# attn x v: v loaded in rows of 32 KiB, sixteen heads at a time, and spread in front of the transposes

## The chip, the core and the metric

One core of a Trainium2 chip runs the whole program. The metric is the time of one execution in microseconds (us) on the device. The kernel before took 1050.37 us, the median of three runs (1050.12 to 1050.52).

Names used below: TensorE (PE) multiplies matrices and transposes them by a matmul against an identity; its weight loads are PEld. VectorE (DVE) and ScalarE (ACT) copy results out of PSUM. GpSimd (POOL) issues most transfers here, and SyncE (SP) the others. [...]

## The reference

```python
# attn_weights: (8, 12, 1024, 1024) float32, v: (8, 12, 1024, 64) float32
np.einsum('bhqs,bhsd->bhqd', attn_weights, v).astype(np.float32)
```

For each of 96 heads a 1024 x 1024 matrix is multiplied with a 1024 x 64 one. `attn` is 403 MB, v and the output 25 MB each.

## The kernel before

**Tiling.** Four heads make one step of the loop, 24 steps in all (`NV`). In a tile of 128 partitions each of the four heads has 32 partitions, and a partition holds 32 consecutive query rows of its head. A step is two *units* of 16 of these rows each (`G` = 16, `NU` = 48 units): the even one (`i == 0`) and the odd one. A unit's part of `attn` is 8 MB in float32, loaded by one transfer on POOL that casts it to bfloat16 on the way (`load_attn`, L344), 64 KiB to a partition, into one of two buffers `abf`.

**A unit on TensorE** (`pe_unit`). It waits for its load and transposes the 16 groups by 64 matmuls (`transpose_g`, L144), two bfloat16 taken as one float32, into four PSUM banks in turn. Copies on DVE (ten groups) and ACT (six) bring them to `at` (L277); a group waits for the copy of the group four before it. Then `transpose_back` (L174) transposes the output `ot` of the unit before by eight matmuls into the banks `px`, from where ACT copies it to `osb` (L258). Then 64 matmuls (L189) form the products of `at` with v (`vbf`) in the banks `po`, and DVE and ACT copy them to `ot` (L289).

**v and its spreading.** The products need v with the sequence on the partitions in an interleaved order. v comes in long rows: with `V8` = 8 heads on 128 partitions, a partition holds 64 consecutive rows of one head, 16 KiB in float32. `spread_v` brings them into place by matmuls against a band matrix `spread`: step b of `VB` = 8 takes the row block b of all 16 partitions of a head and puts it on every eighth partition. It accumulates the steps of a head in one PSUM bank (`po` and `px`, one bank a head); the contraction runs over 32 partitions (`VR`), in which two heads lie, and the other head's weights are zero. The four heads of a step lie on two sets of 32 partitions. The steps are written in pairs of heads, (0, 2) and then (1, 3), so that each matmul is followed by one on the other set. Each head has its own band in `spread`. DVE and ACT cast the four results to `vbf` (L250).

**The order.** All of it is written by hand, engine by engine, with semaphores. In an even unit TensorE transposes `attn` first, then waits for the copies of the products of the unit before (`s_ot`) and for v (`s_vr`), spreads, waits for the four casts (`s_vbf`), transposes back and multiplies. A branch on the loop's counter picks the spread for the step's place in the buffer `vr`.

**Transfers.** POOL issues in program order. Before the loop: the first unit of `attn`, a part of the first v, the second unit. In the loop: in the even unit, where a load of v is due (`V_LOADS`: eight heads for step 2, then sixteen heads for steps 4, 8, ..., 20), it waits for the spread that read the old v last (`s_sp`) and issues that load (L350). Then in each unit it waits until the unit's transposes are done (`s_t`) and issues the `attn` load after next into the buffer that these freed. The first v comes in two halves, one by SP through `osb` with a cast on DVE (L332), one by POOL. Stores of `osb` come in two bursts, after steps 8 and 16, and at the end; TensorE halts half-way through unit 18 and unit 34 until a burst has landed (`s_half`).

## Time and profile before

| | |
|---|---|
| time, median of three runs | 1050.37 us |
| span of the profiled execution | 1048.8 us |
| PE busy | 792.7 us, 76% of the span |
| PEld, DVE, ACT busy | 706.1, 389.3, 469.5 us |
| mean granted TensorE clock | 0.879 |
| HBM read, written | 427.82 MB, 25.17 MB |
| loads of `attn`, 4096 KB landed each | 46, median 29.2 us from issue to landing |
| loads of v, 2048 KB landed each | 5, median 15.8 us |
| spreading (L161), matmuls | 768, TensorE busy 87.0 us |

The profiled execution is read by its span, from its first instruction to its last; what the runs' times have beyond it (1.6 us at the median) lies around that. In a group of the profile stand the line, engine and operation, the shapes, the count, the busy time, the mean length of one instruction in ns, and the idle time just before the group with what ended it. Matmuls overlap in the pipeline, so their mean length times their count is more than their busy time. In the timeline and the chain of waits a row begins with start and length in us.

### The profile page before, as it was taken

Reading aid. Unit: us, or ns where it says so; the run is one execution under the profiler, and the core shown is the slowest. Engines: PE = TensorE matmul, PEld = TensorE weight load, DVE = VectorE, ACT = ScalarE, POOL = GpSimd, SP = SyncE. Lnnn points to the kernel's source line nnn. Section 1 sums busy time; section 2 is a strip of 40 time slices with the busy share of each in tenths; the row PEclk is TensorE's granted clock in tenths of the full one; section 3 lists DMA queues with packets and bytes.
Section 4 is the critical chain, followed back from the end, with each engine's and each line's share of the span. In section 5 each row is a group of like instructions: output and inputs, shape, how many; then the busy total and the mean of one; then the engine's idle time right before and its main releaser. Section 6 shows DMA issues by size and latency. Waiting matters only on the chain.

```text
span 1048.8 us, 17363 instructions
## 1 busy us (share of the span) xinstructions
PE 792.7 (76%) x7304; PEld 706.1 (67%) x7304; DVE 389.3 (37%) x584; ACT 469.5 (45%) x590; POOL 36.9 (4%) x68
## 2 busy tenths in 40 slices
PE   0978788479889393888949789748578884987994
PEld 0777687368778383777838588647567774867884
DVE  1443344234435151343515344324324332533542
ACT  0445355244545251354526355434335443544553
POOL 1000000000000000000000000000000000000000
PEclk9989799798999697889979899988778987998998
DMA  9999999999999999999999999999999999999999
GB/s 216 226 220 217 217 209 217 220 220 216 220 215 207 221 220 379 217 219 210 212 223 220 216 220 217 206 221 220 319 237 219 214 209 223 220 217 219 210 214 400
DMA packets 10662, 239.68 MB, mean 229 GB/s; under 512 B 1056, under 2 KB 1056, under 8 KB 1184
## 3 DMA queue, kind: packets, MB, share of 16 engines
q0 software_dynamic: 10080, 232.26, 98.9%
q1 hardware_dynamic: 576, 7.34, 1.7%
q8 instruction: 3, 0.05, 0.0%
q14 instruction: 3, 0.02, 0.0%
HBM read 427.82 MB, written 25.17 MB: 432 GB/s over the span
## 4 chain that ended last, share of the span: by engine, by line
DMA 71%; PE 26%; issue 1%; POOL 1%; ACT 0%; DVE 0%; SPq 0%; ACTq 0%; POOLq 0%
DMA abf<-in_attn_weights_dram 63%; PE bank L144 22%; DMA out_dram<-osb 8%; PE bank L161 3%; PE bank L189 1%; PE bank L174 0%; POOL vr L350 0%; DVE osb L258 0%; ACT vbf L250 0%; ACT osb L258 0%; POOL abf L344 0%; ACT ot L289 0%; POOL out_dram L358 0%; ACTq L258 0%; SPq L420 0%
## 5 line engine op out<-in xcount | busy, mean ns | idle before, releaser
L144 PE MATMUL bank<-ident,abf 128*128 128x128 f32 x3072 | 428.8, 307 | 213.0 <-DMA abf<-in_attn_weights_dram 189.5
L144 PEld LDWEIGHTS bank<-ident,abf 128*128 128x128 f32 x3072 | 419.1, 212 | 224.7 <-DMA abf<-in_attn_weights_dram 197.7
L277 DVE COPY at<-bank 128x1024 bf16<-128x1024 bf16 x480 | 319.6, 689 | 401.8 <-PE bank L144 395.2
L277 ACT COPY at<-bank 128x1024 bf16<-128x1024 bf16 x288 | 287.9, 1012 | 328.6 <-PE bank L144 328.6
L189 PE MATMUL bank<-at,vbf 128*64 128x256 bf16 x3072 | 225.5, 285 | 0.0
L189 PEld LDWEIGHTS bank<-at,vbf 128*64 128x64 bf16 x3072 | 203.6, 111 | 19.1 <-issue 6.1
L258 ACT COPY osb<-bank 64x512 f32 (+1 forms) x194 | 112.4, 580 | 28.1 <-PE bank L174 25.5
L289 DVE COPY ot<-bank 128x512 f32<-128x512 f32 x48 | 33.2, 692 | 207.1 <-PE bank L189 207.1
L161 PE MATMUL bank<-vr,spread 32*128 32x512 bf16 x768 | 87.0, 375 | 0.5 <-issue 0.2
L289 ACT COPY ot<-bank 128x512 f32<-128x512 f32 x48 | 28.1, 585 | 129.2 <-PE bank L189 129.2
L174 PE MATMUL bank<-ident,ot 128*128 128x128 f32 x392 | 61.3, 307 | 29.3 <-ACT vbf L250 28.7
L174 PEld LDWEIGHTS bank<-ident,ot 128*128 128x128 f32 x392 | 50.3, 157 | 41.4 <-ACT vbf L250 40.5
L161 PEld LDWEIGHTS bank<-vr,spread 32*128 32x128 bf16 x768 | 35.2, 93 | 43.9 <-issue 1.6
L250 ACT CAST vbf<-bank 128x512 bf16<-128x512 f32 x48 | 25.8, 588 | 74.3 <-PE bank L161 74.3
L344 POOL DMA_DIRECT2D abf<-in_attn_weights_dram x50 | 26.9, 537 | 816.1 <-PE bank L144 815.3
L250 DVE CAST vbf<-bank 128x512 bf16<-128x512 f32 x48 | 30.9, 686 | 29.1 <-PE bank L161 29.1
L277 ACT ACT_TABLE_LOAD x12 | 15.4, 1283 | 6.4 <-DMA osb<-in_v_dram 6.3
L350 POOL DMA_DIRECT2D vr<-in_v_dram x6 | 4.0, 675 | 132.9 <-PE bank L161 132.9
L358 POOL DMA_DIRECT2D out_dram<-osb x5 | 3.1, 620 | 7.5 <-ACT osb L258 7.5
L258 DVE COPY osb<-bank 64x512 f32<-64x512 f32 x2 | 1.4, 688 | 3.0 <-PE bank L174 3.0
L325 DVE MEMSET ident<- 128x128 f32 x1 | 0.2, 165 | 6.2 <-DMA osb<-in_v_dram 6.2
L332 DVE CAST vr<-osb 128x1024 bf16<-128x1024 f32 x2 | 2.2, 1138 | 0.0
(9 smaller groups left out, 5.1 us busy)
## 6 DMA issues: line engine op xcount, KB each, us to landing
abf<-in_attn_weights_dram POOLq DMA_DIRECT2D x46, 4096.0 KB, 29.2
vr<-in_v_dram POOLq DMA_DIRECT2D x5, 2048.0 KB, 15.8
out_dram<-osb POOLq DMA_DIRECT2D x1, 8192.0 KB, 39.5
abf<-in_attn_weights_dram POOLq DMA_DIRECT2D x4, 2048.0 KB, 22.8
out_dram<-osb POOLq DMA_DIRECT2D x3, 2048.0 KB, 32.9
out_dram<-osb SPq DMA_DIRECT2D x3, 2048.0 KB, 13.8
out_dram<-osb POOLq DMA_DIRECT2D x1, 4096.0 KB, 41.6
osb<-in_v_dram SPq DMA_DIRECT2D x1, 1024.0 KB, 5.1
```

Of the source, the lines that this page charges most:

```text
L144: last = pe.matmul(out=pt[g % 4][:, k], lhsT=words[:, k], rhs=ident, is_transpose=True, start=(k == 0), stop=(k == KW - 1),)
L161: last = pe.matmul(out=banks[h], lhsT=spread[rows, j, ds(VB - 1 - b, P)], rhs=vr[rows, n // 2, b], start=(b == 0), stop=(b == VB - 1),)
L174: last = pe.matmul(out=px[j0 // 4][:, ds(j * P, P)], lhsT=ot[:, j0 + j], rhs=ident, is_transpose=True, start=(j == 0), stop=(j == 3),)
L189: last = pe.matmul(out=outs, lhsT=vbf[:, 2 * kw + par, h], rhs=at[:, ds(half * GH, GH), kw, ds(h * VP, VP), par], start=(n == 0), stop=(n ...
L250: copy(out=vbf[:, :, h], in_=ps.rearrange("p (k d) -> p k d", k=SB)).then_inc(s_vbf)
L258: last = copy(out=rows[ds(n // 2 % 2 * HP, HP), ds(pp * 2 * G + n % 2 * G, G)].rearrange("p (half j) d -> p j half d", half=2)[:, ds(4 * k ...
L277: ins = copy(out=at[:, g].rearrange("c k j two -> c (k j two)"), in_=bank[g % 4].bitcast(bf16),)
L289: copy(out=ot.rearrange("c j (pp h p) -> c h j pp p", pp=2, h=VH)[:, ds(2 * e, 2)], in_=po[e].rearrange("c (h j p pp) -> c h j pp p", h=2, ...
L332: last = nc.vector.tensor_copy(out=vr_first[:, 0, part], in_=v32[:, part])
L344: pool.dma_start(out=abf[n % 2][:, ds(g0, gn)].rearrange("p g s -> p (g s)"), in_=attn_q[n // 2][:, ds((n % 2 * G + g0) * S, gn * S)],).th ...
L350: pool.dma_start(out=vr[:, ds(q % V_AT_ONCE // 2, fours // 2)].rearrange("p n b x -> p n (b x)"), in_=v_n(q, fours),).then_inc(s_v, 16)
L358: eng.dma_start(out=out_n(q, fours), in_=at_slot, **({"single_packet": True} if eng is pool and fours == 2 else {}),).then_inc(done, 16)
```

## The change

v is loaded sixteen heads at a time (`V16`), each on eight partitions, so that a partition holds 128 rows of one head, 32 KiB in float32, in one row of the transfer instead of two of 16 KiB. Four heads of a step now lie together on one set of 32 partitions (`rows = ds(n * VR, VR)`), and `VB` is 16: sixteen steps a head instead of eight, 64 matmuls for the four heads instead of 32, head after head in the order 0, 2, 1, 3. `spread` is one band of 128 x 2063 for all heads, of which each step takes a window of 128 columns. The first load brings sixteen heads too: a quarter by SP (the same bytes as before), the rest by POOL ahead of the first `attn` load. The loads for steps 4, 8, ..., 20 stay; that for step 2 goes.

In an even unit TensorE now spreads first and then transposes `attn`; the wait for `s_ot` stands ahead of the spread, that for `s_vbf` behind the transposes. DVE and ACT cast the spread results ahead of the unit's copies.

```diff
-    VB = S // (P // V8) // SB
+    V16 = 4 * VH
     VR = 32
+    VB = S // (P // V16) // SB
+    VW = (P - 1) * VB + 1 + 2 * (VB - 1)
...
-    V_LOADS = {2: 2, **{q: V_AT_ONCE for q in range(V_AT_ONCE, NV, V_AT_ONCE)}}
+    V_LOADS = range(V_AT_ONCE, NV, V_AT_ONCE)
...
-    def v_n(q, fours):
-        return v_h[ds(q * VH, fours * VH)].rearrange(
-            "(n eight) (p r) d -> (eight p) n (r d)", eight=V8, p=P // V8
-        )
+    def v_n(q):
+        return v_h[ds(q * VH, V16)].rearrange("h (p r) d -> (h p) (r d)", p=P // V16)
...
-    spread = sb("spread", [P, V8, P + VB - 1], bf16)
+    spread = sb("spread", [P, VW], bf16)
...
-            for pair in ((0, 2), (1, 3)):
+            rows = ds(n * VR, VR)
+
+            for h in (0, 2, 1, 3):
                 for b in range(VB):
-                    for h in pair:
-                        j = n % 2 * VH + h
-                        rows = ds(j * (P // V8) // VR * VR, VR)
-                        last = pe.matmul(
-                            out=banks[h],
-                            lhsT=spread[rows, j, ds(VB - 1 - b, P)],
-                            rhs=vr[rows, n // 2, b],
+                    last = pe.matmul(
+                        out=banks[h],
+                        lhsT=spread[rows, ds((n * VH + h) * P + VB - 1 - b, P)],
+                        rhs=vr[rows, b],
...
         def pe_unit(i, n, both, loaded, it):
 
-            pe.wait_ge(*loaded)
-            for g in range(G):
-                if g == GH:
-                    pe.wait_ge(s_half, n)
-                transpose_g(abf[i], g, n)
-            pe.wait_ge(s_ot, both)
             if i == 0:
+                pe.wait_ge(s_ot, both)
                 pe.wait_ge(s_vr, it)
...
                         spread_v(0, po + px)
+            pe.wait_ge(*loaded)
+            for g in range(G):
+                if g == GH:
+                    pe.wait_ge(s_half, n)
+                transpose_g(abf[i], g, n)
+            if i == 0:
                 pe.wait_ge(s_vbf, it * 4)
+            else:
+                pe.wait_ge(s_ot, both)
...
-                for g in mine:
-                    copy_g(g, of_t + (n * per + count_of(g)))
                 if n % 2 == 0:
                     spread_copy(e, po[e], of_sp + (2 * n + 2 * e + 2))
                     spread_copy(2 + e, px[e], of_sp + (2 * n + 2 * e + 2))
+                for g in mine:
+                    copy_g(g, of_t + (n * per + count_of(g)))
...
+        late = ds(V_SYNC, VB * SB * D - V_SYNC)
+        pool.dma_start(out=vr_flat[:, late], in_=v_n(0)[:, late]).then_inc(s_v0, 16)
         load_attn(0)
-        pool.dma_start(out=vr_first[:, 1], in_=v_first[:, 1]).then_inc(s_v0, 16)
         load_attn(1)
```

On TensorE, at the end of an even unit's transposes before the change (`s_cp11` counts the copies of group 11; the branches pick one of four spreads):

```order
L144 MATMUL bank<-ident,abf 128x128 [waits s_cp11]
L144 MATMUL bank<-ident,abf 128x128 x3
L206 ISA
L210 ISA [waits s_vr,s_ot]
L210 COMPARE_AND_BRANCH
L211 COMPARE_AND_BRANCH
L161 MATMUL bank<-vr,spread 128x512 x32
```

On TensorE, at the head of the loop's body after the change:

```order
L231 ISA
L202 ISA [waits s_vr,s_ot]
L202 COMPARE_AND_BRANCH
L203 COMPARE_AND_BRANCH
L159 MATMUL bank<-vr,spread 128x512 x64
```

The wait for v and for the products' copies, the branches and the spread have moved from behind the transposes to the start of the even unit, and the spread has 64 matmuls. Further on, behind the last of the four spreads, after the change:

```order
L159 MATMUL bank<-vr,spread 128x512 x64
L210 UNCONDITIONAL_BRANCH
L212 REGISTER_ALU
L144 MATMUL bank<-ident,abf 128x128 [waits s_abf0]
L144 MATMUL bank<-ident,abf 128x128 x15
```

The transposes with their wait for the load (`s_abf0`) now follow the spread, with no wait for the casts between the two.

On POOL, from the making of the band matrix to the first load of sixteen heads in the loop, before the change:

```order
L382 AFFINE_SELECT spread<-spread 128x1080 [waits s_const]
L344 DMA abf<-in_attn_weights_dram 128x16384 [waits s_t_dve] x2
L350 DMA vr<-in_v_dram 128x4096 [waits s_sp]
L344 DMA abf<-in_attn_weights_dram 128x16384 [waits s_t_dve] x4
L350 DMA vr<-in_v_dram 128x2x4096 [waits s_sp]
```

On POOL, from its first transfer to the same place, after the change:

```order
L364 DMA vr<-in_v_dram 128x6144
L344 DMA abf<-in_attn_weights_dram 128x16384 x2
L367 NO_OP [waits DMAHW0_49,Pool_sequencer_49]
L369 ISA [waits s_const]
L369 AFFINE_SELECT ident<-ident 128x128
L380 AFFINE_SELECT spread<-spread 128x2063 [waits s_const]
L344 DMA abf<-in_attn_weights_dram 128x16384 [waits s_t_dve] x6
L350 DMA vr<-in_v_dram 128x8192 [waits s_sp]
```

The load of v for step 2 is gone, that for step 4 is one row of 8192 elements a partition instead of two of 4096, and the first v stands in front of the first `attn` load. A load of v still waits for the spread of the step before (`s_sp`), which now comes ahead of that unit's transposes (`s_t_dve`).

## The prediction

> **What bounds the kernel now.** I read the page from the DMA side first: how full the queues are, what the chain that ended last is made of, and what ended TensorE's idle time.

> ```profile
> DMA  9999999999999999999999999999999999999999
> q0 software_dynamic: 10080, 232.26, 98.9%
> DMA 71%; PE 26%; issue 1%; POOL 1%; ACT 0%; DVE 0%; SPq 0%; ACTq 0%; POOLq 0%
> L144 PE MATMUL bank<-ident,abf 128*128 128x128 f32 x3072 | 428.8, 307 | 213.0 <-DMA abf<-in_attn_weights_dram 189.5
> ```

> The 16 DMA engines are never free, and TensorE idles 213.0 us in front of the transposes, nearly all of it for a landing load of `attn`. So the DMA queue sets the time. Its pace is read from the chain of waits, where a load's start plus its length is its landing.

> ```profile
> 555.07 29.18 DMA abf<-in_attn_weights_dram
> ...
> 594.70 28.24 DMA abf<-in_attn_weights_dram
> ...
> 632.72 28.83 DMA abf<-in_attn_weights_dram
> ...
> 675.32 34.59 DMA abf<-in_attn_weights_dram
> ```

> The landings are at 584.25, 622.94, 661.55 and 709.91: two loads (a pair of units, four heads) take 38.65, so one takes 19.32, and a pair with a load of v among it takes 48.36, so that load takes 9.71. By bytes it should take half an `attn` load (2048 KB against 4096 KB as they land), 9.66. That bounds the first edit: **rows of 32 KiB instead of 16 KiB** can win about 0.05 us a load, 0.3 us over the run.

> **What TensorE has left.** A pair of units on TensorE, from its timeline:

> ```profile
> 458.70 9.80 PE L144 MATMUL bank<-ident,abf 128*128 128x128 f32 x64 [4.78 <-DMA abf<-in_attn_weights_dram]
> 468.44 3.63 PE L161 MATMUL bank<-vr,spread 32*128 32x512 bf16 x32
> 473.26 1.93 PE L174 MATMUL bank<-ident,ot 128*128 128x128 f32 x8 [1.19 <-ACT vbf L250]
> 475.12 5.21 PE L189 MATMUL bank<-at,vbf 128*64 128x256 bf16 x64
> 480.25 7.95 PE L144 MATMUL bank<-ident,abf 128*128 128x128 f32 x64
> 488.04 1.04 PE L174 MATMUL bank<-ident,ot 128*128 128x128 f32 x8
> 489.01 4.48 PE L189 MATMUL bank<-at,vbf 128*64 128x256 bf16 x64
> ```

> A unit without spreading takes 13.24 from 480.25 to the end of its products at 493.49 when the clock is full, and 15.1 when its transposes start at half clock (9.80 for 7.95). The pair's idle time is 213.0/24 = 8.9 us. That is all the cover there is.

> **The steps of spreading.** Before, 32 matmuls a pair of units; now 64, and all four heads read the same 32 partitions. What one step costs is in the first 0.2 us of a spread, seen through two narrow windows of the timeline:

> ```profile
> 468.44 0.39 PE L161 MATMUL bank<-vr,spread 32*128 32x512 bf16 x2
> 468.44 0.60 PE L161 MATMUL bank<-vr,spread 32*128 32x512 bf16 x4
> ```

> Up to 468.60 two have started, up to 468.80 two more, and the pair's end moved by 0.21: two heads on two bands of 32 partitions run at once, and a band takes its next step every 0.21 (16 steps in 3.63 less the last one's tail of about 0.17 is 0.216 each). With one band for all heads, nothing runs at once: 64 x 0.216 = **13.8 us** for 3.63. The nearest bounds: 64 x 0.113 = 7.3, if steps of one band overlapped as those of two do; 27.3 at half clock, since the same eight transposes of L174 take 1.93 after a spread and 1.04 without one.

> **Which clock it gets.** This decides the sum, so I looked at stretches of 3.41 us, the raster on which the granted clock changes (columns: stretch, length, TensorE busy and matmuls, granted clock, DMA share, GB/s).

> ```profile
> 77.40:80.82 3.42, 2.61 (x26) 1.00 1.20 259
> 80.82:84.23 3.41, 3.02 (x16) 0.50 0.85 183
> 507.49:510.90 3.41, 2.71 (x26) 1.00 1.29 279
> 510.90:514.32 3.42, 2.93 (x36) 1.00 0.84 182
> 527.97:531.38 3.41, 2.09 (x32) 1.00 0.85 183
> 531.38:534.79 3.41, 0.00 (x0) 1.00 1.20 259
> 435.80:439.22 3.42, 1.02 (x14) 1.00 0.90 192
> 439.22:442.63 3.41, 3.31 (x16) 0.50 0.89 192
> ```

> Each two rows are a stretch and the one after it. The first four hold spreading alone in the first of the two: 2.61 us of it lose the clock in the next stretch, 2.71 keep it. The next four hold products alone (L189): 2.09 keep it, 1.02 lose it. So a stretch needs some amount of work, and spreading counts for less than it is busy. How much less, from two stretches with spreading and then transposes of L174, filtered to each of the two lines:

> ```profile
> 374.42:377.83 3.41, 1.45 (x14) 0.99 1.29 279
> 722.49:725.90 3.41, 1.52 (x16) 1.00 1.29 279
> ...
> 374.42:377.83 3.41, 0.76 (x7) 0.99 1.29 279
> 722.49:725.90 3.41, 0.69 (x6) 1.00 1.29 279
> 377.83:381.24 3.41, 3.41 (x28) 0.51 0.85 183
> 725.90:729.30 3.40, 3.40 (x52) 1.00 0.86 183
> ```

> 1.45 of spreading and 0.76 of L174 lose it, 1.52 and 0.69 keep it: 1.49 s + 0.72 t is the limit, and so is 2.66 s. Hence s = 0.62 t, limit 1.65 us of full-array work. Two bands out of four count as 0.62 of four. I read that as a share of the array, so one band counts about 0.31, and a stretch filled with it 3.41 x 0.31 = 1.06, under 1.65: **the clock drops inside the new spread**. The other end: if one band counts as much as two, 2.1, it stays.

> [...]

> How long the full clock lasts: the stretch in which the spread begins also holds the end of the products and a gap of 0.9 (the product's copy, whose row is below, with handing over and the branches; I take 0.9, bounds 0.65 and 2). With u of it left for the spread it counts (3.41 - 0.9 - u) + 0.31 u; that reaches 1.65 for u under 1.25, and then one more full stretch follows. Over all positions that is (1.25 x 4.0 + 2.16 x 2.3)/3.41 = 2.95 us, 13.7 steps. The other 50.3 take 0.427: 21.5. **Spread: 24.4 us.**

> ```profile
> 453.96 0.58 ACT L289 COPY ot<-bank 128x512 f32<-128x512 f32 x1 [2.38 <-PE bank L189]
> L174 PE MATMUL bank<-ident,ot 128*128 128x128 f32 x392 | 61.3, 307 | 29.3 <-ACT vbf L250 28.7
> ```

> **What moves.** The spread now stands in front of the even unit's transposes. Gone: the wait for the casts of v, 28.7/24 = 1.2 a pair, since the transposes now lie over them; the casts delay ACT's first copy by half a microsecond, which is caught up. New: the wait for the copies of the products (0.9), behind which stand the spread, the transposes of L144 that free `abf`, POOL's wait for them, and so the load after next. On POOL v's load is now issued a unit's transposes ahead of the `attn` load instead of just ahead of it. It queues behind a load already issued, so it costs nothing while the queue has slack. The even transposes begin at half clock.

> **The sum.** Pair: 0.9 + 24.4 + 15.1 + 13.3 = **53.7 us** on TensorE, against 38.65 to 48.36 of the queue. TensorE becomes the bound, and the queue waits for it. 23 pairs: 1235.

> ```profile
> 1.33 23.86 DMA abf<-in_attn_weights_dram
> 8.21 1.97 POOL L382 TENSOR_SCALAR_AFFINE_SELECT spread<-spread 128x1080 bf16<-128x1080 bf16 x1
> out_dram<-osb POOLq DMA_DIRECT2D x1, 8192.0 KB, 39.5
> 1029.33 4.42 PE bank L189 x64
> ...
> 1036.24 0.69 DVE osb L258
> ```

> First pair: the rest of the first v (1536 KB, 7.3 at the queue's pace) stands before the first `attn` load, which lands at 25.2 now and so begins at 5.9; v is there at 5.9 + 7.3 + 0.5 = 13.7 (the band matrix, twice as wide, takes 4 instead of 1.97 on POOL and is there at about 13); its spread is at half clock throughout, 27.3; with 15.1 and 13.3 that is 69.4. Bursts of stores: 39.5 from issue to landing with a load of 19.3 ahead; the load behind it lands 62 after the issue and is wanted at 59, so 3. Tail: before, 15.05 from the end of the last products (1033.75) to 1048.8, with five stores in the queue; now only the last store is left by then, so 3.2 of copies, a quarter of the 8192 KB burst's own 19.5 to 20 (4.9) and about 2.5 of start and end: 10.6. Span: 69.4 + 1235 + 3 + 10.6 = 1318. The profiled span before is 1048.8, the median of the runs 1050.4, so 1.6 lie around it: **1320 us**.

> **The rivals.**
> - *The clock stays full.* Pair: 0.9 + 13.8 + 13.24 + 13.3 = 41.2. Four pairs are 165 on TensorE and 4 x 38.65 + 9.71 = 164 in the queue: neither has slack, each late even load leaves the queue empty for 1 to 3 us, and waits for bursts are not caught up. Ten such bubbles and some 5 of lag at the end: 1070 (1055 to 1100, with a slightly lighter band up to 1110). For it: the kept clock after 2.71 of spreading; against it: the count of 0.62.
> - *Not slower.* The spread is hidden in TensorE's wait for `attn`, 8.9 a pair. It adds 24.4 - 3.63 and gives back 1.2; covered only up to a spread of about 10.5 us, that is under 0.165 a step. At 0.113 it would be 1050, less the 0.3 of longer rows and a microsecond of fewer, fuller transfers at best: 1049. For it: pairs did run at 0.113. Against it: they had two bands.

> That the change does not do what it says I exclude: the order shows 64 steps on one band and loads of 8192 elements.

> **Chances.** The clock drops 0.86, full clock 0.09, hidden 0.05. The drop's own range: a full clock for 5 us of each spread with a short gap gives 51.2 a pair, 1262; a spread nearly all at half clock with transposes of 10.4 and a longer gap gives 56.7, 1390. I give that 0.93 of the case, 0.80 in all, and so the range is 1262 to 1390. A measurement of this kernel tells about 0.2% (2.1 us) from no change. Faster 0.01, same 0.04, slower 0.95.

> **What would show it.** Right: spread matmuls that end one by one, x64 in 22 to 27 us; granted clock 0.50 in stretches inside them and a mean of 0.7 to 0.8 over the span; idle before L144 for `attn` nearly gone; DMA share down to about 0.8; a chain of TensorE. Wrong: a spread of 13.8 at clock 1.00 (then 0.31 is too small), one of 7 to 8 (then bands are not what runs at once), or landings still 38.65 apart with TensorE waiting for them.

## The result, and the profile after

| | before | after |
|---|---|---|
| median of four runs | 1050.44 us | 1350.70 us |
| span of the profiled execution | 1048.8 us | 1348.4 us |
| mean granted TensorE clock | 0.879 | 0.761 |
| PE busy | 792.7 us (76%) | 1296.5 us (96%) |
| share of 16 DMA engines, q0 | 98.9% | 78.4% |
| spreading on TensorE | 87.0 us, 768 matmuls | 616.3 us, 1536 matmuls |

The ratio of the runs is 1.286, its 95% interval 1.284 to 1.288. The forecast was 1320 us, with a range of 1262 to 1390.

From the page of the changed kernel, the lines that answer those of before: the two strips of 40 slices, the queue's share, the chain by engine, and the groups of the spread (now L159) and of the transposes.

```profile
PEclk9958678587696786967858678587696876967859
DMA  9978498695868959959778595895995987659495
q0 software_dynamic: 9296, 232.26, 78.4%
PE 93%; DMA 4%; issue 1%; ACT 1%; DVEq 0%; DVE 0%; POOLq 0%; SPq 0%
L159 PE MATMUL bank<-vr,spread 32*128 32x512 bf16 x1536 | 616.3, 594 | 41.1 <-ACT ot L289 27.2
L144 PE MATMUL bank<-ident,abf 128*128 128x128 f32 x3072 | 428.7, 306 | 2.3 <-DMA abf<-in_attn_weights_dram 2.3
```

TensorE's wait for landing `attn` has gone from 189.5 us to 2.3, and the chain is made of TensorE, where it was made of DMA. The queue now has holes. One spread lasts 616.3/24 = 25.7 us where it lasted 3.6. One pair of units, from TensorE's timeline:

```profile
401.19 25.49 PE L159 MATMUL bank<-vr,spread 32*128 32x512 bf16 x64 [1.09 <-ACT ot L289]
426.61 9.69 PE L144 MATMUL bank<-ident,abf 128*128 128x128 f32 x64
436.14 1.04 PE L171 MATMUL bank<-ident,ot 128*128 128x128 f32 x8
437.11 4.48 PE L186 MATMUL bank<-at,vbf 128*64 128x256 bf16 x64
441.52 8.09 PE L144 MATMUL bank<-ident,abf 128*128 128x128 f32 x64
...
456.20 25.89 PE L159 MATMUL bank<-vr,spread 32*128 32x512 bf16 x64 [1.32 <-ACT ot L289]
```

From spread to spread it is 55.0 us, with no wait but the one for the products' copies. The clock in that spread, in stretches of 3.41 us on the raster of its changes (stretch, length, TensorE busy and matmuls, granted clock, DMA share, GB/s):

```profile
399.85:403.26 3.41, 2.32 (x13) 1.00 0.98 211
403.26:406.68 3.42, 3.42 (x10) 0.50 1.16 249
406.68:410.09 3.41, 3.41 (x9) 0.50 0.71 154
...
427.15:430.56 3.41, 3.41 (x18) 0.50 0.85 144
430.56:433.98 3.42, 3.42 (x30) 1.00 1.01 216
```

The spread begins at 401.19 in a stretch at full clock. At its end the clock halves, though TensorE is busy without a break from there on: eight matmuls in 3.41 us, 0.427 each (the counts of 10 and 9 take in those that lie across an end of the stretch). It comes back at 430.56, after a stretch that is all transposes.

### The profile page after: what moved, and what is told of

Same layout as the page of the kernel before. It is cut to its first block, busy times and chain, and to the rows that moved or that the text cites. A ratio compares the mean times of both kernels' runs of the same rounds, so it can differ in the third digit from the quotient of the medians.

```text
span 1348.4 us, 18897 instructions
## 1 busy us (share of the span) xinstructions
PE 1296.5 (96%) x8072; PEld 866.3 (64%) x8072; DVE 390.2 (29%) x584; ACT 470.8 (35%) x590; POOL 36.1 (3%) x67
## 3 DMA queue, kind: packets, MB, share of 16 engines
q0 software_dynamic: 9296, 232.26, 78.4%
## 4 chain that ended last, share of the span: by engine, by line
PE 93%; DMA 4%; issue 1%; ACT 1%; DVEq 0%; DVE 0%; POOLq 0%; SPq 0%
PE bank L159 44%; PE bank L144 31%; PE bank L186 15%; DMA abf<-in_attn_weights_dram 4%; PE bank L171 3%; ACT ot L289 1%; DMA vr<-in_v_dram 1%; DVEq L136 0%; DVE osb L258 0%; SPq L411 0%; POOLq L448 0%; POOLq L136 0%
## 5 line engine op out<-in xcount | busy, mean ns | idle before, releaser
L159 PE MATMUL bank<-vr,spread 32*128 32x512 bf16 x1536 | 616.3, 594 | 41.1 <-ACT ot L289 27.2
L159 PEld LDWEIGHTS bank<-vr,spread 32*128 32x128 bf16 x1536 | 209.3, 137 | 432.6 <-issue 408.1
L144 PEld LDWEIGHTS bank<-ident,abf 128*128 128x128 f32 x3072 | 419.6, 215 | 27.2 <-issue 24.7
L144 PE MATMUL bank<-ident,abf 128*128 128x128 f32 x3072 | 428.7, 306 | 2.3 <-DMA abf<-in_attn_weights_dram 2.3
L250 ACT CAST vbf<-bank 128x512 bf16<-128x512 f32 x48 | 25.8, 589 | 622.5 <-PE bank L159 622.5
L186 PE MATMUL bank<-at,vbf 128*64 128x256 bf16 x3072 | 215.0, 278 | 0.0
L186 PEld LDWEIGHTS bank<-at,vbf 128*64 128x64 bf16 x3072 | 196.7, 108 | 13.3 <-DVE at L277 8.0
L250 DVE CAST vbf<-bank 128x512 bf16<-128x512 f32 x48 | 30.9, 686 | 346.3 <-PE bank L159 346.3
L258 ACT COPY osb<-bank 64x512 f32 (+1 forms) x194 | 112.5, 580 | 4.2 <-PE bank L171 0.8
L289 DVE COPY ot<-bank 128x512 f32<-128x512 f32 x48 | 33.2, 691 | 127.3 <-PE bank L186 127.3
L289 ACT COPY ot<-bank 128x512 f32<-128x512 f32 x48 | 28.1, 585 | 113.6 <-PE bank L186 113.6
L171 PE MATMUL bank<-ident,ot 128*128 128x128 f32 x392 | 50.9, 273 | 0.7 <-ACT ot L289 0.7
L171 PEld LDWEIGHTS bank<-ident,ot 128*128 128x128 f32 x392 | 45.0, 143 | 0.9 <-ACT ot L289 0.9
L380 POOL TENSOR_SCALAR_AFFINE_SELECT spread<-spread 128x2063 bf16<-128x2063 bf16 x1 | 2.7, 2721 | 0.1
L258 DVE COPY osb<-bank 64x512 f32<-64x512 f32 x2 | 1.4, 689 | 3.0 <-PE bank L171 3.0
## 6 DMA issues: line engine op xcount, KB each, us to landing
out_dram<-osb POOLq DMA_DIRECT2D x1, 8192.0 KB, 40.1
```

Source lines behind the costliest of these rows:

```text
L144: last = pe.matmul(out=pt[g % 4][:, k], lhsT=words[:, k], rhs=ident, is_transpose=True, start=(k == 0), stop=(k == KW - 1),)
L159: last = pe.matmul(out=banks[h], lhsT=spread[rows, ds((n * VH + h) * P + VB - 1 - b, P)], rhs=vr[rows, b], start=(b == 0), stop=(b == VB - 1),
L171: last = pe.matmul(out=px[j0 // 4][:, ds(j * P, P)], lhsT=ot[:, j0 + j], rhs=ident, is_transpose=True, start=(j == 0), stop=(j == 3),)
L186: last = pe.matmul(out=outs, lhsT=vbf[:, 2 * kw + par, h], rhs=at[:, ds(half * GH, GH), kw, ds(h * VP, VP), par], start=(n == 0), stop=(n ...
L250: copy(out=vbf[:, :, h], in_=ps.rearrange("p (k d) -> p k d", k=SB)).then_inc(s_vbf)
L258: last = copy(out=rows[ds(n // 2 % 2 * HP, HP), ds(pp * 2 * G + n % 2 * G, G)].rearrange("p (half j) d -> p j half d", half=2)[:, ds(4 * k ...
```

## The experiments

Three theories stood against one another. **A**: the steps follow one another on one band, and the granted clock goes by the share of the array that works, so that one band does not hold it. **B**: the granted clock goes by the time in which matmuls run, and is lost to the gap ahead of the spread. **C**: the loss comes from the new order. Each experiment ran beside the kernel before on the same chip (1050.3 to 1050.5 us).

### All 128 partitions in each step

```diff
-            rows = ds(n * VR, VR)
+            rows = ds(0, P)
```

> The changed kernel, with one line of the spread altered: each step contracts over all 128 partitions instead of the 32 of its band (the band matrix has zeros for the other 96, so the sums are the same). Steps still follow one another on the same part of the array, so nothing else becomes concurrent. Theory A (the clock gate counts the share of the array that works, one band about 0.3 of four): a step now counts fully, the clock stays at 1.00 through the spread, spread 13.8 to 14.0 us instead of 25.7, pair 41.5 us, TensorE and the DMA queue about equal, time 1065 to 1085 us. Theory B (the gate counts the time in which matmuls run; the clock is lost to the gap of 1.2 us ahead of the spread): no difference, spread 25 to 26, about 1350. Theory C (the loss comes from the spread standing ahead of the transposes): no difference either, about 1350.

Measured: 1077.4 us, ratio 1.026 (1.0245 to 1.028). From its timeline and its windows, a spread and the clock inside one:

```profile
464.53 13.99 PE L159 MATMUL bank<-vr,spread 128*128 128x512 bf16 x64 [1.23 <-ACT ot L289]
...
404.15:417.97 13.82, 13.82 (x64) 1.00 0.90 322
```

The same 64 steps, in the same order, behind the same gap, with the same loads: 13.99 us for 25.7, all at full clock. This takes 273 of the 300 us away by one line that gives the array more to do. B and C fall, since neither gap nor order has changed. The 13.99 is also the price of 64 steps one behind the other, 0.216 each.

### Two bands in each step

```diff
-            rows = ds(n * VR, VR)
+            rows = ds(n // 2 * (P // 2), P // 2)
```

> As the run over 128 partitions, but each step contracts over 64 partitions, two bands. Theory A: a step counts as a pair of heads did before the change, 0.62; a stretch of 3.41 us full of it (2.1) holds the clock, but the stretch in which the spread begins also has the gap of 1.2 us, and falls short for about a third of the positions; once at half clock 0.62 is too little to come back. So some spreads of 13.9 us at full clock and some of 22 to 25, 1080 to 1250 us. Theories B and C: about 1350, as with 32 partitions.

Measured: 1189.3 us, the median of four runs (1154.0 to 1205.6), ratio 1.132 (1.126 to 1.138). Two spreads of the profiled execution, which is the fastest of the four, from the timeline:

```profile
378.26 25.60 PE L159 MATMUL bank<-vr,spread 64*128 64x512 bf16 x64 [1.32 <-ACT ot L289]
...
491.54 13.98 PE L159 MATMUL bank<-vr,spread 64*128 64x512 bf16 x64 [1.18 <-ACT ot L289]
```

There are two kinds of spread and none between: of the 23 after the first, 16 take 13.98 or 13.99 and 7 take 25.6 to 26.0. The sixteen held a clock that was there; the seven did not get it back before their end. This fits the prediction's estimate of 0.62: by it a stretch full of such steps comes to 2.1 at full clock, and to half of that at half clock, where a step of the changed kernel took 0.427 us and one at full clock 0.216. The position goes with it, as forecast, but for an overlap from 1.59 to 1.71: the seven that lost the clock began with 1.59 to 1.97 us of their stretch left, the sixteen that kept it with at most 1.71 or at least 2.81. That this is also why the kernel's runs are spread over 50 us was not shown: the mean granted clock falls from 0.909 in the fastest of the four to 0.867 in the slowest, but only the fastest has a trace.

### The order alone, on the kernel before

```diff
-            pe.wait_ge(*loaded)
-            for g in range(G):
...
             if i == 0:
+                pe.wait_ge(s_ot, both)
                 pe.wait_ge(s_vr, it)
...
+            pe.wait_ge(*loaded)
+            for g in range(G):
```

> The kernel before, with the order on TensorE, DVE and ACT alone taken from the change: the spread (two bands, 32 matmuls, rows of 16 KiB) ahead of the even unit's transposes, its casts ahead of the copies. Theories A and B: TensorE keeps slack (a pair of about 33 us against 38.65 of the queue), the queue stays full, 1048 to 1053 us, same. Theory C: most of the 300 us, at least 1100.

Measured: 1052.4 us, ratio 1.002 (1.001 to 1.003). C falls here too. The 2 us are most likely those of the first v: its second half still comes behind the first `attn` load here, so the first spread, and with it the transposes, start later. In the trace the third `attn` load is issued at 45.3 us, where it was 35.3, and lands at 69.2, where it was 67.0. That was not tried by itself.

### The change with the old order

```diff
+            pe.wait_ge(*loaded)
+            for g in range(G):
...
+            pe.wait_ge(s_ot, both)
             if i == 0:
-                pe.wait_ge(s_ot, both)
                 pe.wait_ge(s_vr, it)
...
-            pe.wait_ge(*loaded)
-            for g in range(G):
```

(The transposes stand ahead of the spread again, and the casts behind the copies.)

> The changed kernel with the order of before: transposes first, then the one-band spread of 64 steps with its casts waited for. Theory A: the spread loses its clock all the same, a little later since it starts without a gap (full clock for about 4.3 us, 20 steps), 23.2 us; with the casts' wait and a half-clock start of the products a pair of 53 to 54, 1290 to 1335 us. Theory B: no gap ahead of the spread, so the clock stays, spread 13.9, 1065 to 1100. Theory C: 1050 to 1100.

Measured: 1403.9 us, ratio 1.337 (1.331 to 1.342). B falls again: without a gap ahead of it the spread still loses its clock (23.90 us below, for 13.98 to 13.99 at full clock). But all three forecasts missed, and the order of the change turns out to be worth 53 us to it. From this kernel's chain of waits, a pair with a load of v:

```profile
664.74 23.90 PE bank L159 x64
688.64 0.28 issue
688.93 0.52 POOL vr L347
689.45 31.16 DMA abf<-in_attn_weights_dram
```

The spread itself is near the 23.2 us expected. What I had left out is POOL: in these pairs it waits for the spread, issues the load of v, and only then the `attn` load whose buffer had been free since 664.7. That load lands at 720.61, and TensorE waits for it. TensorE's six waits for `attn`, the first of the run and these, sum to 82.3 us.

### That order, with POOL's two loads exchanged

```diff
+            pool.wait_ge(s_t[True], (n + 1) * PER_DVE)
+            load_attn(n + 2)
             if i == 0 and q + 1 in V_LOADS:
                 pool.wait_ge(s_sp, 4 * (q + 1))
                 load_v(q + 1)
-            pool.wait_ge(s_t[True], (n + 1) * PER_DVE)
-            load_attn(n + 2)
```

> The run with the one-band spread behind the transposes, with one exchange on POOL: the attn load is issued first, then POOL waits for the spread and issues the load of v. If the pairs with a load of v took 67 instead of 53 us there because POOL held the attn load back behind its wait for the spread: these five pairs fall to about 53, 1325 to 1345 us. If the bytes of v or their place in the queue cost it: 1390 to 1410 as without the exchange.

Measured: 1348.4 us (1344.7 and 1352.0), ratio 1.284 (1.275 to 1.292). From the timeline of POOL, the same place of the program:

```profile
648.33 0.53 POOL L341 DMA_DIRECT2D abf<-in_attn_weights_dram  x1 [12.77 <-PE bank L144]
671.76 0.53 POOL L347 DMA_DIRECT2D vr<-in_v_dram  x1 [22.91 <-PE bank L159]
```

The `attn` load is out 23 us ahead of that of v, and TensorE's waits for `attn` fall from 82.3 us in six to 31.9 in one, the first. So the 55 us were POOL's program order. With it out of the way the old and the new order cost the changed kernel the same (1348 and 1351). The time lies 3 us above the expected range: a pair is 54.2 on average, not 53.

### Four bands at once

```diff
-            rows = ds(n * VR, VR)
...
-            for h in (0, 2, 1, 3):
-                for b in range(VB):
+            for b in range(VB):
+                for h in (0, 2, 1, 3):
+                    rows = ds(h * VR, VR)
...
-                        lhsT=spread[rows, ds((n * VH + h) * P + VB - 1 - b, P)],
+                        lhsT=spread[rows, ds((h * VH + n) * P + VB - 1 - b, P)],
```

> The changed kernel with its 64 steps, rows of 32 KiB, loads and order, but step b of the four heads goes to four different bands, one behind the other: head h of step n is taken from band h (head 4h + n of the sixteen) instead of band n. So each output is formed with v of another head of the sixteen, the work is the same. Theory A: four steps run at once on four bands, the spread takes 16 x 0.216 and a tail, 3.6 us, at full clock; a pair is 32 to 33 us on TensorE against 38.65 of the queue, the queue bounds again: 1048 to 1051 us, at most a microsecond under the kernel before, which is all that the longer rows can give. If the 64 steps themselves, or the loads, or the order cost the time: 1070 or more.

Measured: 1050.2 us, ratio 0.9998 (0.9989 to 1.0007). From its timeline, and from its chain of waits the landings two loads apart, the last with a load of v between:

```profile
455.97 3.63 PE L158 MATMUL bank<-vr,spread 32*128 32x512 bf16 x64 [1.18 <-ACT ot L289]
...
613.89 28.38 DMA abf<-in_attn_weights_dram
...
652.11 28.75 DMA abf<-in_attn_weights_dram
...
691.70 37.49 DMA abf<-in_attn_weights_dram
```

64 steps in 3.63 us, as long as 32 on two bands. Number of steps, rows of 32 KiB, sixteen heads a load, and order together cost nothing measurable; what costs is that the four heads of a step lie on one band. The landings (642.27, 680.86, 729.19) are 38.59 and 48.33 apart, so the load of v takes 9.74 us in its long rows, against 9.71 in short ones: the rows give nothing that these rows could show.

### Full steps among the band's, one of eight and three of eight

```diff
-            rows = ds(n * VR, VR)
...
+                    rows = ds(0, P) if b % 8 in (2, 5, 7) else ds(n * VR, VR)
```

(Three of eight; the other has `b % 8 == 7`.)

> As the run over 128 partitions, but only every eighth step contracts over 128 partitions, the other seven over their band of 32. Theory A with counts that add up: 0.31 + 0.69/8 = 0.40 a step, 1.35 us in a stretch of 3.41, under the limit of 1.65: the clock drops inside every spread, 1320 to 1360 us. If any full-array work in a stretch holds the clock: 1070 to 1085.

> As before, with three of eight steps over 128 partitions. Theory A: 0.31 + 0.69 x 3/8 = 0.57 a step, 1.94 us in a stretch, over the limit; the stretch in which the spread begins falls short for about half of the positions, and then the spread stays at half clock. So spreads of 13.6 to 14 us beside others of 22 to 26, 1130 to 1270 us, more than with two bands (0.62). If counts do not add up that way: 1075 or 1350.

Measured, one run each: 1378.6 and 1423.2 us. Both are slower than the change. The first lies above its forecast of 1320 to 1360, and the second contradicts its own. The first spread of each, which is at half clock from end to end, shows why (timelines of one of eight, of three of eight and of the changed kernel):

```profile
13.83 14.07 PE L159 MATMUL bank<-vr,spread 32*128 32x512 bf16 x31 [13.83 <-issue]
...
42.79 5.49 PE L144 MATMUL bank<-ident,abf 128*128 128x128 f32 x35
...
14.14 5.11 PE L159 MATMUL bank<-vr,spread 32*128 32x512 bf16 x10 [14.14 <-issue]
...
46.69 1.70 PE L144 MATMUL bank<-ident,abf 128*128 128x128 f32 x7
...
41.34 6.94 PE L144 MATMUL bank<-ident,abf 128*128 128x128 f32 x43
```

From the first step to the transposes it is 28.96, 32.55 and (from 13.92) 27.42 us: 15 changes between 32 and 128 rows add 1.5, 47 add 5.1, so each change cost about 0.1 us here.

With such pauses fewer steps fit into a stretch than I had counted. Three stretches in a row inside one spread of three of eight:

```profile
366.51:369.92 3.41, 3.41 (x13) 1.00 0.76 163
369.92:373.33 3.41, 3.41 (x13) 1.00 1.38 298
373.33:376.75 3.42, 3.42 (x8) 0.50 0.71 153
```

Eight steps with six changes take 8 x 0.216 + 6 x 0.1 = 2.3 us, so by this estimate a stretch holds about 12 steps instead of 16, and by the prediction's weights, estimates too (1 for a full step, 0.31 for one of a band), they count 1.4 us and not 1.94. The first of these stretches keeps the clock and the second, with the same steps, loses it: by these weights an estimate of the limit is 1.4, where the prediction's had been 1.65. One of eight comes to 1.2 in the same way; it lost the clock in all 23 spreads after the first, at the latest behind one full stretch. So by these estimates it was the pauses that the two forecasts had left out.

### Two heads full, then two on their band

```diff
-            rows = ds(n * VR, VR)
...
             for h in (0, 2, 1, 3):
+                rows = ds(0, P) if h in (0, 2) else ds(n * VR, VR)
```

> The changed kernel with heads 0 and 2 of each spread contracting over all 128 partitions and then heads 1 and 3 over their band of 32, so that there is one change of the row count in a spread. Theory A: the first 32 steps (6.9 us) hold the clock, the band's steps hold it for the rest of a stretch and at most one more (3 to 5 us), the remaining 2 to 4 us of work run at half clock: spread 15.5 to 18, transposes behind it with a half-clock start, pair 45 to 47, 1115 to 1165 us. If the clock were lost by the gap ahead of the spread, or by zeros in the weights: the first 32 steps at half clock too, 1300 or more.

Measured: 1144.7 us, ratio 1.090 (1.087 to 1.093). From its timeline (the row names the first step's form):

```profile
536.77 15.26 PE L159 MATMUL bank<-vr,spread 128*128 128x512 bf16 x64 [1.05 <-ACT ot L289]
...
551.96 8.29 PE L144 MATMUL bank<-ident,abf 128*128 128x128 f32 x51
```

With one change of rows in a spread the forecast holds: the full steps hold the clock behind the same gap, and the band's steps lose it late. In the profiled execution 50 to 59 of the 64 steps run at full clock in all spreads but the first, so the loss comes 18 to 27 steps into the band's part. The latest loss is in a spread that begins at 908.41, so that its full steps end near 915.3:

```profile
914.75:918.16 3.41, 3.41 (x17) 1.00 1.34 288
918.16:921.58 3.42, 3.42 (x18) 1.00 0.80 172
921.58:924.99 3.41, 3.41 (x14) 0.50 1.12 240
```

The first of these stretches holds 0.57 us of full steps and then only the band, by the same weights 0.57 + 2.7 x 0.31 = 1.4, and the clock stays; the next is all band, 1.06, and the clock drops. This estimate too lies under 1.65.

## Why the prediction was right, point by point

**The bound changes sides: right.** The queue's slack shows as holes in the DMA strip, and TensorE's waits for `attn` are gone.

**One step after the other, 13.8 us: right.** 13.98 to 13.99 where the clock is full, and 27.4 for the first spread at half clock, forecast 27.3. The four bands, 64 steps in 3.63 us, show that concurrency, not the count of steps, is the price.

**The clock drops inside the spread: right, and it is most of the loss.** 273 of 300 us go with it. The reading that the granted clock goes by the share of the array at work, taken from a handful of stretches before the change, was borne out by three sizes: 32 partitions lose the clock in each of the 23 spreads after the first, 64 in 7 of 23, 128 in none. The sizes behind it are off. By the prediction's weights a count of 1.4 kept the clock in two runs (three of eight, two heads full), while spreading before the change lost it with 2.61 x 0.62 = 1.62. The weight of 0.62 came from taking the transposes of L174 as full work, which no run shows. With the plain shares of the array as weights, a quarter for one band and a half for two, the counts come together: before the change 1.31 lost the clock (2.61 us of spreading) and 1.36 kept it (2.71), 1.25 kept it with two heads full, and 1.34 did both with three of eight. From these stretches an estimate of the limit is 1.3 us of full-array work in a stretch, and one band's 3.41/4 = 0.85 lies far under it, as 1.06 lay under 1.65. No run was made to test either estimate. Matmuls that followed one another without a break did not keep the clock here: in the stretch from 403.26 on TensorE is busy for 3.42 of 3.42 us at a granted clock of 0.50.

**How long the full clock lasts: mis-sized.** I took 13.7 of 64 steps, an average over all positions of the spread on the raster, and 24.4 us. Measured are 9.0 steps on average (4 to 13) over the 23 spreads after the first, and (616.3 - 27.5)/23 = 25.6 us. The forecast gave a further full stretch at full clock to a spread that begins with under 1.25 us of its stretch left. None got it: the three that came so late (at 125.56, 733.28 and 1119.09, with 1.22, 1.07 and 0.97 left) lost the clock at the stretch's end. With the measured gap of 1.18 instead of 0.9 the prediction's own count puts that mark at 0.84 instead of 1.25, and no spread began so late. For the positions are not spread evenly: most pairs take about 54.9 us, close to 16 stretches of 3.413, 54.6, so each spread begins 0.2 to 0.4 later in its stretch than the one before. After the latest ones the clock comes back a stretch later, the pair takes longer (1119.09 to 1175.58 is one of 56.5) and the next spread begins early in its stretch again. Which part of the shortfall belongs to the gap and which to the positions no run separates. Together, 25.6 for 24.4, they are 23 x 1.2 = 28 us, nearly all of what the forecast is short of.

**The gap ahead of the spread: mis-sized.** 27.2/23 = 1.18 us for 0.9; 6 us in all.

**First pair, bursts, tail: right.** The first pair's products end at 69.4, as forecast; the burst costs 2.3 us of waiting at unit 19 for 3; the tail from the last products is 9.6 us for 10.6. The 2.5 us of start and end in that sum is the author's estimate, which no run shows by itself; the last store, issued 3.2 us after the last products, took 6.3 us to its landing, where the forecast had 7.4.

**Rows of 32 KiB give almost nothing: right.** Forecast at most 0.05 us a load; 9.74 against 9.71.

**The moved order costs nothing of its own: right, but not for all the reasons given.** I counted POOL's earlier issue of v as free. It is more than that: in the old order, which does without it, the five pairs with a load of v cost 53 us more.

**The rivals.** The full-clock rival, put at 1070 (1055 to 1100), is the run over 128 partitions: 1077. The hidden one is the run with four bands: 1050. So each was sized about right, and the profile had told which would come. The hidden rival's limit of 10.5 us a spread does not follow from the terms beside it (8.9 + 3.63 + 1.2 is 13.7); no run tests it.

No version here beats the kernel before. The best, four bands at once, equals it, because the queue bounds both; as it stands it leaves out the layout of v that would give each output its own head.

## What to carry to other kernels

Before doubling the steps of a small-contraction matmul, look at which partitions neighbouring steps read: here 64 steps on four bands of 32 took 3.63 us, 64 steps one behind the other took 13.98 to 13.99 at full clock, and the layout that put all operands of the stage on one band took that away. A stage that used a quarter of the array had the clock halved for itself and for the first of what followed (transposes of 9.69 us for 8.09), here within 3 us of its start; where its other rows multiplied by zeros, the same steps kept the clock and took 0.216 us each, as the steps of a band did before the change. And a wait that is moved on one engine is to be followed onto the queues that wait for it: here a load of 4096 KB stood behind a wait on POOL that had nothing to do with it.

## What the runs showed of the hardware

Two bands kept a full clock in 16 spreads of 23 in one execution (13.98 or 13.99 us), but where it was lost they stayed at half clock to the end of the spread, 7 times of 7 (25.6 to 26.0 us). This looks like two limits, a higher one to regain the clock than to keep it. But at half clock a step took 0.427 us for 0.216, so a stretch did half the work, and counted by work one limit may be enough. Before the change, with transposes of L144 alone at half clock (each two rows are a stretch and the one after it):

```profile
801.00:804.41 3.41, 2.41 (x11) 0.50 0.85 183
804.41:807.83 3.42, 3.42 (x18) 0.50 1.20 259
196.93:200.34 3.41, 2.80 (x14) 0.51 0.85 183
200.34:203.76 3.42, 3.42 (x31) 1.00 1.29 278
```

A change between matmuls of 32 and of 128 rows cost about 0.1 us in the first spreads of the two runs with full steps among the band's (1.5 us for 15 changes, 5.1 for 47). The traces show that there is a pause, but not what makes it.
